# Second mixer: the context keys' gates to the context's end, by a scan on VectorE in place of eight levels on GpSimd

## The chip, the cores and the metric

The kernel runs on one core of a Trainium2 chip. The metric is the device time of one execution in microseconds (us), as the median of several runs. The engines are called as the profile calls them: PE (TensorE matmul), PEld (its weight loads), DVE (VectorE), ACT (ScalarE), POOL (GpSimd) and SP (the queue that issues most transfers).

## The reference

The network has four layers (two blocks of two) over 256 context tokens and 256 latent tokens of width 1024. The change is in the second mixer, a gated linear recurrence in two directions, with eight heads of width 128. Only the latent tokens' output is needed there.

```python
def _directional_scan(q, k, v, g, n_ctx, reverse):
    """One scan direction: context scanned alone from a zero state, latent scan starts from the final context state."""
...
    o_ctx, s_ctx = _chunk_gla(seg(q, c_sl), seg(k, c_sl), seg(v, c_sl), seg(g, c_sl), s0)
    o_lat, _ = _chunk_gla(seg(q, t_sl), seg(k, t_sl), seg(v, t_sl), seg(g, t_sl), s_ctx)
...
def _odd_mixer(h_ctx, h_lat, w_in, lower_bounds, layer, out_norm, ctx_out):
...
    for d, f in enumerate((f_fwd, f_bwd)):
        log_f = jnp.logaddexp(jnp.log(lb[d]), jnp.log1p(-lb[d]) + jax.nn.log_sigmoid(_heads(f, HGRN_HEADS).astype(jnp.float32)))
        k = -jnp.expm1(log_f)
        dirs.append(_directional_scan(q, k, i, log_f, n_ctx, reverse=(d == 1)))
    o_lat = _gated_readout(dirs[0][1] + dirs[1][1], og[:, :, n_ctx:], out_norm)
```

Here `_chunk_gla` is the recurrence S_t = diag(exp(g_t)) S_{t-1} + k_t v_t^T, o_t = S_t^T q_t. For a latent token, each context key therefore counts with the product of all gates that stand between it and the end of the context (for the reverse direction, its beginning), for each of the 128 features of its head.

## The kernel before

Activations are kept feature by feature (128 partitions) with tokens along the row. The linear layers work in fp32 split in two: for every weight tile that a transfer brings (`raw`), ACT rounds a high part (`hi`, L195) and DVE subtracts it from the tile to get the low part (`lo`, L196); PE then makes three products (L205 to L207, or L277 to L280 where tokens are the output's rows).

`odd_mixer` handles the eight heads as four pairs. `proj(p)` makes the gates of pair p for the latent (`al`) and the context tokens (`ac`), the keys `Kl` and `Kc` (one minus the gate, L814 and L816 on DVE), and the queries `q`; `late(p)` makes the output gates and the values. `hgrn_pair` then does the recurrence of one pair. Its latent part runs over eight levels of a dyadic tree. At each level, ACT gathers keys (`KC`, L898), PE multiplies keys by queries (L901), DVE puts the masked result into the score tile `S` (L903), and DVE multiplies the gates of the level into `Q2` (L915) and `Kl` (L906). DVE also makes the next level's products of neighbouring gates (`tot`, L921). The next level's matmuls need the `Q2` of the level before.

Beside this, POOL runs the same tree over the context: at each level L916 multiplies into `Kc` the gates of the level, and L921 makes the next products from `ac`. After eight levels, every context key holds all gates up to the context's end; L936 and L937 multiply `Kc` by the queries. POOL also makes `ks`, the sum of both directions' keys (L881), at the head of a pair.

The program's order is proj(0), late(0), proj(1), pair 0, late(1), proj(2), pair 1, proj(3), and then pairs 2 and 3 taking turns level by level, with late(2) and late(3) after twelve steps. The tile framework lays out each engine's instructions from this order, but lets an instruction that is ready pass earlier ones that are not. So the `tot` products and the context's levels of a pair, which depend only on its gates, stand in the queues of DVE and POOL right behind its projection, ahead of the levels of the pair before.

Of the kernel before, what the change touches and what calls it, by code (L numbers as in the profile page):

```python
# [9 lines left out]
F32 = mybir.dt.float32  # L10
# [3 lines left out]
ALU = mybir.AluOpType  # L14
# [3 lines left out]
P = 128  # L18
# [19 lines left out]
def vw(ap, off, dims):  # L38
    return bass.AP(ap.tensor, ap.offset + off, [ap.ap[0]] + [list(d) for d in dims])
# [89 lines left out]
class Kern:  # L129
# [741 lines left out]
    def hgrn_pair(self, p, al, ac, Kl, Kc, Q2, q, V, sog, gain, mix):  # L871
        nc = self.nc
        mm = nc.tensor.matmul
        DS = 512

        def g2(name):
            return mix.tile([P, 2, 256], F32, tag=name, name=self.n(name), bufs=2)

        S = g2("S")
        ks = mix.tile([P, 2, 256], F32, tag="S256", name=self.n("ks"), bufs=2)  # L880
        nc.gpsimd.tensor_tensor(ks, Kl[:, 0], Kl[:, 1], ALU.add)  # L881
        ps = self.psum("pa")
        for h in range(2):
            for tt in range(2):
                ts = slice(tt * P, (tt + 1) * P)
                mm(ps[:, h * 256 + tt * P:h * 256 + (tt + 1) * P], ks[:, h, ts], q[:, h, ts], start=True, stop=True)
        nc.scalar.copy(S.rearrange("p h n -> p (h n)"), ps)
        for d in range(2):
            nc.vector.tensor_tensor(Q2[:, d], q, al[:, d], ALU.mult)
        tl = al.rearrange("p d h n -> p (d h n)")  # L890
        tc_ = ac.rearrange("p d h n -> p (d h n)")
        for lev in range(8):
            m = 1 << lev
            nb = DS // (2 * m)
            pat = [[2 * m, nb], [DS + m, 2], [1, m]]
            if lev < 7:
                KC = g2("KC").rearrange("p h n -> p (h n)")
                nc.scalar.copy(vw(KC, 0, [[2 * m, nb], [m, 2], [1, m]]), vw(Kl, 0, pat))  # L898
                ps = self.psum("pa")
                for b in range(4):  # L900
                    mm(ps[:, b * P:(b + 1) * P], KC[:, b * P:(b + 1) * P],  # L901
                       vw(Q2, b * P, [[2 * m, 64 // m], [DS + m, 2], [1, m]]), start=True, stop=True)
                nc.vector.copy_predicated(S.rearrange("p h (t i) -> p (h t) i", t=2),  # L903
                                          self.masks[:, lev, None, :].to_broadcast([P, 4, P]),
                                          ps.rearrange("p (t i) -> p t i", t=4))
                nc.vector.tensor_tensor(vw(Kl, 0, pat), vw(Kl, 0, pat), self.dyadic(m, DS, nb, tl, "k"), ALU.mult)  # L906
            else:
                S128 = g2("S128")
                ps = self.psum("pa")
                for h in range(2):  # L910
                    o = h * 256
                    mm(ps[:, o + P:o + 256], Kl[:, 0, h, :P], Q2[:, 1, h, P:], start=True, stop=True)
                    mm(ps[:, o:o + P], Kl[:, 1, h, P:], Q2[:, 0, h, :P], start=True, stop=True)
                nc.scalar.copy(S128.rearrange("p h n -> p (h n)"), ps)
            nc.vector.tensor_tensor(vw(Q2, 0, pat), vw(Q2, 0, pat), self.dyadic(m, DS, nb, tl, "q"), ALU.mult)  # L915
            nc.gpsimd.tensor_tensor(vw(Kc, 0, pat), vw(Kc, 0, pat), self.dyadic(m, DS, nb, tc_, "k"), ALU.mult)  # L916
            if lev < 7:
                for w, eng in (("l", nc.vector), ("c", nc.gpsimd)):
                    t2 = mix.tile([P, 2, nb], F32, tag=f"tot{w}{lev}", name=self.n("tot"), bufs=2)
                    pr = vw(tl if w == "l" else tc_, 0, [[DS // m, 2], [2, nb], [1, 2]])  # L920
                    eng.tensor_tensor(t2, pr[:, :, :, 0], pr[:, :, :, 1], ALU.mult)  # L921
                    t2 = t2.rearrange("p d n -> p (d n)")
                    if w == "l":
                        tl = t2
                    else:
                        tc_ = t2
            yield
        tag = "pl" if p > 1 else "pb"
        ss = self.psum("pb")
        oS = []  # L930
        for h in range(2):
            ps = self.psum(tag)
            for j in range(2):
                js = slice(j * P, (j + 1) * P)
                o = ps[:, j * 256:(j + 1) * 256]
                mm(o, Kc[:, 0, h, js], Q2[:, 1, h], start=True, stop=False)  # L936
                mm(o, Kc[:, 1, h, js], Q2[:, 0, h], start=False, stop=True)  # L937
            S256 = mix.tile([P, 512], F32, tag="S256", name=self.n("S256"), bufs=2)
            nc.scalar.copy(S256, ps)
            po = self.psum("pa")  # L940
            vs = slice((2 * p + h) * P, (2 * p + h + 1) * P)
            for j in range(2):
                mm(po[:, :256], V[:, j, vs], S256[:, j * 256:(j + 1) * 256], start=j == 0, stop=False,
                   skip_group_check=True)
            for tt in range(2):
                ts = slice(tt * P, (tt + 1) * P)
                mm(po[:, ts], V[:, 2 + tt, vs], S[:, h, ts], start=False, stop=False, skip_group_check=True)
                mm(po[:, ts], V[:, 3 - tt, vs], S128[:, h, ts], start=False, stop=True, skip_group_check=True)
            oS.append(self.gated_readout_rows(po[:, :256], h, gain, mix, ss))
            yield  # L950
        r = self.sm.tile([P, 8], F32, tag="rs16", name=self.n("rs"))
        self.rstd_rows(ss[:, :4], P, 4, r[:, :4])
        yield
        for h in range(2):
            bc = self.psum(tag)
            for tt in range(2):
                mm(bc[:, tt * P:(tt + 1) * P], r[:, tt * 2 + h:tt * 2 + h + 1].to_broadcast([P, P]), self.ident,
                   start=True, stop=True)
            hd = 2 * p + h
            nc.vector.tensor_tensor(oS[h], oS[h], bc[:, :256], ALU.mult)  # L960
            nc.gpsimd.tensor_tensor(sog[:, hd], oS[h], sog[:, hd], ALU.mult)
# [1172 lines left out]
```

## Time and profile before

| | |
|---|---|
| median of 3 runs | 2568.2 us (2568.14 to 2576.02) |
| the profiled execution's own time | 2566.27 us |
| its span in the trace | 2563.7 us |
| PE busy | 2414.7 us (94%) |
| DVE busy | 1518.1 us (59%), 2897 instructions |
| ACT busy | 971.3 us (38%) |
| POOL busy | 503.0 us (20%), 648 instructions |
| mean granted clock of PE | 0.966 |

A busy share says how long an engine had an instruction in work. PE's share is near full, so that what counts is where PE is idle and which engine it waits for there. The second mixer lies between about 890 and 1185 us of the span. The profiled execution's own time is 2.6 us above its span, which is what lies around it, and 1.9 us below the median of the runs.

### The profile page before, as it was taken

The numbers are of one execution on the slowest core, as the hardware profiler recorded it, in microseconds if no ns is written. First come the engines' busy times: TensorE is split into PE (matmuls) and PEld (weight loads), VectorE is DVE, ScalarE is ACT, GpSimd is POOL, SyncE is SP. The second block draws the span as 40 slices with busy tenths as digits, with TensorE's granted clock in tenths as the row PEclk, the third lists the DMA queues.
The fourth block names the chain that finished last, engine by engine and source line by source line (L and its number), as shares of the span: only waits on it lengthen the run. The fifth ranks groups of instructions, "written<-read, shape, count | busy, mean of one in ns | idle before, by whom it ended". The sixth has DMA issues, their size and how long they took to land.

```text
span 2563.7 us, 40161 instructions
## 1 busy us (share of the span) xinstructions
PE 2414.7 (94%) x15813; PEld 1970.4 (77%) x15813; DVE 1518.1 (59%) x2897; ACT 971.3 (38%) x1591; POOL 503.0 (20%) x648
## 2 busy tenths in 40 slices
PE   6999989999999998889999999999999999948999
PEld 5885566888888688887799696546888888627999
DVE  5545436777853656673655533654688734585666
ACT  5523323322222433333444444443423224534543
POOL 2810012556630233230100100110100000360000
PEclk8999999999999999999999999989999999989999
DMA  8326673555552332123855431003365533976554
GB/s 279 122 95 230 226 279 108 160 163 167 161 145 91 106 124 67 59 82 136 282 178 182 154 110 60 9 17 105 111 188 181 165 99 104 200 254 212 156 181 149
DMA packets 162924, 378.04 MB, mean 147 GB/s; under 512 B 24144, under 2 KB 70096, under 8 KB 162608
## 3 DMA queue, kind: packets, MB, share of 16 engines
q1 hardware_dynamic: 159728, 368.27, 45.0%
q0 software_dynamic: 3008, 7.21, 1.0%
q8 instruction: 124, 2.03, 0.3%
q14 instruction: 64, 0.52, 0.1%
HBM read 344.75 MB, written 30.67 MB: 146 GB/s over the span
## 4 chain that ended last, share of the span: by engine, by line
PE 79%; DVE 10%; DMA 4%; ACT 3%; issue 2%; POOL 1%; SPq 0%; DVEq 0%; ACTq 0%; POOLq 0%
PE pl L205 18%; PE pl L206 18%; PE pl L207 17%; PE pm L329 3%; PE pl L984 2%; PE pa L77 2%; DVE lo L196 2%; DMA mcol<-ada_t 2%; PE pl L279 1%; PE pl L280 1%; DVE pm L395 1%; PE pl L277 1%; PE pb L77 1%; PE pa L661 1%; PE pl L1006 1%
## 5 line engine op out<-in xcount | busy, mean ns | idle before, releaser
L195 ACT CAST hi<-raw 128x1024 fp32r<-128x1024 f32 (+4 forms) x393 | 400.4, 1020 | 847.1 <-PE pl L206 555.0
L196 DVE TENSOR_TENSOR lo<-raw,hi 128x1024 fp32r<-128x1024 f32 (+4 forms) x393 | 496.6, 1265 | 332.2 <-ACT hi L195 330.2
L206 PE MATMUL pl<-X,hi 128*128 128x256 f32 (+1 forms) x2032 | 649.2, 321 | 6.2 <-POOL X L490 5.7
L205 PE MATMUL pl<-X,hi 128*128 128x256 f32 (+1 forms) x2032 | 651.3, 322 | 1.8 <-ACT X L487 1.8
L207 PE MATMUL pl<-X,lo 128*128 128x256 f32 (+1 forms) x2032 | 647.6, 320 | 0.8 <-DVE lo L196 0.7
L206 PEld LDWEIGHTS pl<-X,hi 128*128 128x128 f32 x2032 | 392.6, 194 | 37.4 <-POOL X L490 8.7
L205 PEld LDWEIGHTS pl<-X,hi 128*128 128x128 f32 x2032 | 391.9, 194 | 36.3 <-issue 6.9
L207 PEld LDWEIGHTS pl<-X,lo 128*128 128x128 f32 x2032 | 392.5, 193 | 31.5 <-issue 4.9
L206 PE MATMUL pl<-hl,hi 128*128 128x256 f32 (+1 forms) x1071 | 326.8, 306 | 6.7 <-DVE hl L1713 6.6
L205 PE MATMUL pl<-hh,hi 128*128 128x256 f32 (+1 forms) x1071 | 329.5, 309 | 3.4 <-ACT hh L1712 3.2
L207 PE MATMUL pl<-hh,lo 128*128 128x256 f32 (+1 forms) x1071 | 325.9, 305 | 0.0
L205 PEld LDWEIGHTS pl<-hh,hi 128*128 128x128 f32 x1071 | 202.4, 189 | 25.6 <-issue 7.1
L206 PEld LDWEIGHTS pl<-hl,hi 128*128 128x128 f32 x1071 | 202.6, 189 | 18.9 <-DVE hl L1713 8.7
L207 PEld LDWEIGHTS pl<-hh,lo 128*128 128x128 f32 x1071 | 202.7, 189 | 10.5 <-issue 0.4
L205 PE MATMUL pl<-M,hi 128*128 128x256 f32 (+1 forms) x416 | 125.4, 303 | 7.4 <-ACT hi L195 6.4
L1505 POOL TENSOR_TENSOR Ec<-PGr,bc 128x576 f32<-128x576 f32 x64 | 95.5, 1503 | 169.8 <-DMA bc<-s_w 89.0
L329 PE MATMUL pm<-mraw,s_cc 128*32 128x512 f32 x576 | 115.7, 606 | 11.3 <-DMA mraw<-ada_w 10.9
L207 PE MATMUL pl<-M,lo 128*128 128x256 f32 (+1 forms) x416 | 122.2, 295 | 1.2 <-DVE lo L196 1.2
L206 PE MATMUL pl<-M,hi 128*128 128x256 f32 (+1 forms) x416 | 122.8, 296 | 0.2 <-DVE M L856 0.2
L1726 DVE TENSOR_TENSOR y<-y,pl 128x256 f32<-128x256 f32 (+1 forms) x86 | 45.1, 525 | 115.9 <-PE pl L207 115.5
L490 POOL TENSOR_TENSOR X<-nt,X 128x256 fp32r<-128x256 f32 x48 | 37.5, 781 | 382.7 <-ACT nt L489 382.7
L395 DVE SCALAR_TENSOR_TENSOR pm<-mcol,mrow 128x512 f32<-128x512 f32 x128 | 89.2, 697 | 34.0 <-DMA mcol<-ada_t 21.7
(515 smaller groups left out, 3753.5 us busy)
## 6 DMA issues: line engine op xcount, KB each, us to landing
mraw<-mod_w SPq DMA_DIRECT2D x96, 512.0 KB, 5.5
raw<-f_u SPq DMA_DIRECT2D x88, 512.0 KB, 4.3
mraw<-ada_w SPq DMA_DIRECT2D x64, 512.0 KB, 6.3
raw<-p_u SPq DMA_DIRECT2D x64, 512.0 KB, 3.7
raw<-p_d SPq DMA_DIRECT2D x64, 512.0 KB, 3.6
raw<-ow_fm SPq DMA_DIRECT2D x32, 512.0 KB, 3.3
mcol<-ada_t SPq DMA_DIRECT2D x64, 256.0 KB, 3.0
raw<-f_d SPq DMA_DIRECT2D x32, 448.0 KB, 3.3
```

What stands on the lines that cost most here:

```text
L77: K.nc.tensor.matmul(self.ps[32 * j:32 * j + 32, :N], K.ones[:rows, :32], self.sq[:rows, :N], start=k < 4, stop=k + 4 >= self.kt, skip_gro ...
L195: nc.scalar.copy(hi, raw)
L196: nc.vector.tensor_tensor(lo, raw, f32(hi), ALU.subtract)
L205: mm(out, w[0][:, kw, wsl], xh, start=first and a == 0, stop=False, skip_group_check=True)
L206: mm(out, w[0][:, kw, wsl], xl, start=False, stop=False, skip_group_check=True)
L207: mm(out, w[1][:, kw, wsl], xh, start=False, stop=last and a == nk - 1, skip_group_check=True)
L329: nc.tensor.matmul(ps[32 * j:32 * j + 32, :], s[:, k, :], raw[:, jj * 512:(jj + 1) * 512], start=k == 0, stop=k == KT - 1, skip_group_chec ...
L395: nc.vector.scalar_tensor_tensor(self.psum("pm"), buf[:, n % 2], 1.0, s[:, v], ALU.mult, ALU.mult, accum_out=(dst if h else part)[:, v, j: ...
L490: nc.gpsimd.tensor_tensor(lo[:, k, a:b], t, f32(hi[:, k, a:b]), ALU.subtract)
L984: nc.tensor.matmul(ps[:, :nk], q[:, tt * P:(tt + 1) * P], k[:, :nk], start=True, stop=True)
L1505: nc.gpsimd.tensor_tensor(Ec[i], ff[i], cs[i], ALU.mult)
L1726: nc.vector.tensor_tensor(y[:, c, a0:b0], y[:, c, a0:b0], ps, ALU.add)
```

## The change

POOL's eight levels over the context go. In place of them, DVE scans the context's gates `ac` in place: for each head and direction one `tensor_tensor_scan` over 255 tokens, whose state is multiplied by each gate in turn (and by a column of ones, which changes nothing). For one direction it goes forwards, for the other backwards. Two scans (both heads) of one direction are issued at level 3, those of the other at level 5. After each two, one multiplication on POOL puts the products into `Kc`. The latent part's tree and its `tot` products on DVE stay as they were.

```diff
-        tc_ = ac.rearrange("p d h n -> p (d h n)")
         for lev in range(8):
...
             nc.vector.tensor_tensor(vw(Q2, 0, pat), vw(Q2, 0, pat), self.dyadic(m, DS, nb, tl, "q"), ALU.mult)
-            nc.gpsimd.tensor_tensor(vw(Kc, 0, pat), vw(Kc, 0, pat), self.dyadic(m, DS, nb, tc_, "k"), ALU.mult)
             if lev < 7:
-                for w, eng in (("l", nc.vector), ("c", nc.gpsimd)):
-                    t2 = mix.tile([P, 2, nb], F32, tag=f"tot{w}{lev}", name=self.n("tot"), bufs=2)
-                    pr = vw(tl if w == "l" else tc_, 0, [[DS // m, 2], [2, nb], [1, 2]])
-                    eng.tensor_tensor(t2, pr[:, :, :, 0], pr[:, :, :, 1], ALU.mult)
-                    t2 = t2.rearrange("p d n -> p (d n)")
-                    if w == "l":
-                        tl = t2
-                    else:
-                        tc_ = t2
+                t2 = mix.tile([P, 2, nb], F32, tag=f"totl{lev}", name=self.n("tot"), bufs=2)
+                pr = vw(tl, 0, [[DS // m, 2], [2, nb], [1, 2]])
+                nc.vector.tensor_tensor(t2, pr[:, :, :, 0], pr[:, :, :, 1], ALU.mult)
+                tl = t2.rearrange("p d n -> p (d n)")
+            if lev in (3, 5):
+
+                d = lev // 2 - 1
+                for h in range(2):
+                    a = vw(ac, d * DS + h * 256 + 255 * d, [[1 - 2 * d, 255]])
+                    nc.vector.tensor_tensor_scan(a, a, self.ones[:, :1].to_broadcast([P, 255]), 1.0, ALU.mult, ALU.mult)
+                ks, gs = slice(1 - d, 256 - d), slice(d, 255 + d)
+                nc.gpsimd.tensor_tensor(Kc[:, 1 - d, :, ks], Kc[:, 1 - d, :, ks], ac[:, d, :, gs], ALU.mult)
             yield
```

## Rows read from the trace of the kernel before

**Rows 1.** Waits of PE, 890 to 1180 us: total, times, longest (us).
```profile
PE pa L901 <- DVE Q L915: 15.3, 3, 7.5
PE pa L901 <- DVE S L903: 8.1, 1, 8.1
PE pl L279 <- DVE lo L196: 3.7, 1, 3.7
PE pl L207 <- DVE lo L196: 0.7, 1, 0.7
```

**Rows 2.** Busy time by stretch: first, second, fourth wait, each with the stretch behind.
```profile
core 0: us, PE busy (x) PEld busy (x) DVE busy (x) ACT busy (x) POOL busy (x), PEclk, DMA share, GB/s
913.00:920.60 7.60, 3.19 (x26) 2.83 (x24) 7.53 (x9) 2.27 (x4) 7.60 (x5) 0.98 0.22 69
920.60:924.00 3.40, 3.40 (x17) 3.40 (x18) 3.40 (x4) 0.86 (x2) 3.40 (x3) 0.54 0.49 154
969.80:977.30 7.50, 0.02 (x1) 0.00 (x1) 7.36 (x10) 0.00 (x0) 7.42 (x9) 0.84 0.38 117
977.30:982.00 4.70, 4.67 (x23) 4.70 (x24) 4.70 (x6) 1.46 (x2) 2.06 (x2) 0.52 0.09 37
...
1102.50:1110.60 8.10, 0.03 (x1) 0.00 (x0) 8.00 (x10) 0.53 (x1) 8.10 (x9) 0.63 0.22 65
1110.60:1115.50 4.90, 4.89 (x25) 4.89 (x26) 4.90 (x5) 1.30 (x2) 4.78 (x4) 0.56 0.00 0
```

**Rows 3.** DVE in order of time, second wait: start, duration, operation.
```profile
962.74 1.13 DVE L814 TENSOR_SCALAR Kc<-sg,lbt 128x256 f32<-128x256 f32 x1
...
964.49 2.55 DVE L921 TENSOR_TENSOR tot<-al 128x512 f32<-128x512 f32 x1
...
967.50 2.56 DVE L196 TENSOR_TENSOR lo<-raw,hi 128x1024 fp32r<-128x1024 f32 x1
...
975.02 0.71 DVE L903 COPY_PREDICATED S<-masks,pa 128x512 f32<-128x512 int32 x1
975.63 1.55 DVE L915 TENSOR_TENSOR Q<-Q,al 128x512 f32<-128x512 f32 x1
...
980.52 0.68 DVE L915 TENSOR_TENSOR Q<-Q,tot 128x512 f32<-128x512 f32 x1
981.12 0.68 DVE L906 TENSOR_TENSOR Kl<-Kl,tot 128x512 f32<-128x512 f32 x1
```

**Rows 4.** POOL in order of time, second wait: the first of its 15 instructions.
```profile
962.58 1.14 POOL L921 TENSOR_TENSOR tot<-ac 128x512 f32<-128x512 f32 x1 [33.66 <-DVE ac L816]
```

**Rows 5.** Single lines: duration least/median/most (ns), first and last start.
```profile
L814 DVE TENSOR_SCALAR Kc<-sg,lbt x16: 344/348/1170, 895.8 to 1095.8; 128x256 f32<-128x256 f32 x16
L670 DVE TENSOR_TENSOR tot<-gla_a x2: 679/804/929, 92.0 to 98.3; 128x512 f32<-128x512 f32 x2
L684 DVE TENSOR_TENSOR K<-K,tot x2: 425/425/425, 228.3 to 239.6; 128x256 f32<-128x256 f32 x2
L196 DVE TENSOR_TENSOR lo<-raw,hi x393: 426/1225/3689, 42.8 to 2552.4; 128x1024 fp32r<-128x1024 f32 x171, 128x896 fp32r<-128x896 f32 x16, 128x672 fp32r<-128x672 f32 x4, 128x544 fp32r<-128x544 f32 x4
L916 POOL TENSOR_TENSOR Kc<-Kc,tot x28: 1052/1320/4903, 912.7 to 1113.5; 128x512 f32<-128x512 f32 x28
```

**Rows 6.** DVE in order of time, fourth wait: `Kc`, eleven more, then `S`.
```profile
1095.78 1.13 DVE L814 TENSOR_SCALAR Kc<-sg,lbt 128x256 f32<-128x256 f32 x1
...
1109.84 0.71 DVE L903 COPY_PREDICATED S<-masks,pa 128x512 f32<-128x512 int32 x1
```

**Rows 7.** Waits of SP's queue, 890 to 1000 us.
```profile
SPq L257 <- DVE lo L196: 77.7, 16, 10.5
...
SPq L326 <- PE pm L329: 4.1, 1, 4.1
```

**Rows 8.** Busy time of one stretch among the levels.
```profile
984.00:986.00 2.00, 2.00 (x19) 1.89 (x18) 2.00 (x4) 0.41 (x1) 0.00 (x0) 1.00 0.00 0
```

## Prediction

> **What bounds the kernel now.** I read the page first: PE is busy for 94% of the span, so a change on DVE and POOL can pay only where PE stands still. I therefore asked next for PE's own waits in the second mixer. Four places make up nearly all of them [rows 1]: one wait of 3.7 us (with 0.7 us just ahead) for a `lo`, two of 7.5 us for `Q`, and one of 8.1 us for `S`. All four are waits for DVE. The reader should see that none is a wait for POOL: nobody on PE waits for the context's levels, and counted by waits POOL's work is free.
>
> The view by stretches shows what the waits have in common [rows 2]. In each, DVE is busy throughout and so is POOL, while PE is at work for 3.19 of 7.6 us in the first and for about nothing in the others (the third, at 1045, repeats the second in every column to within 0.03 us and isn't shown). PE's idle time there is 4.4 + 7.5 + 7.5 + 8.1 = 27.5 us. [...] That costs 3.4 x 0.46 = 1.6 us, 4.7 x 0.48 = 2.3 us, the same for the third, and 4.9 x 0.44 = 2.2 us: 8.4 us more. All four together are 35.9 us. This is the most that a cure of these waits could give.
>
> Why is DVE late? The order of time in the second wait tells it [rows 3, 4]. POOL starts on the context's levels at 962.58, as soon as the gates are there, and works almost without a pause until 979.4 (2.06 us into the stretch behind the wait [rows 2]). In that time the same DVE instructions that are short elsewhere are long. A `lo` takes 2.56 us, against a median of 1.22; a `Q` takes 1.55 us, and 0.68 once POOL has stopped; `Kc` takes 1.13 us, against 0.35; the first `tot` takes 2.55 us, where the other mixer's instruction of the same shape took as little as 0.68 [rows 3, 5]. The copy under a mask, which reads its data from PSUM, takes 0.71 us in the middle of it. So DVE's products of two SBUF tensors, and some copies with a factor, wait for POOL's instructions, and PE waits for DVE. POOL's levels are not free after all.
>
> **What is removed.** For each pair, eight multiplications into `Kc` (L916) and seven products (L921) leave POOL: 60 instructions in four pairs. For the second wait, I go through DVE's queue from 962.74 to the start of `S` at 975.02, which is 12.3 us [rows 3]. Undisturbed, `Kc` and `Kl` are 0.35 each; the first `tot` is 0.68; the six smaller ones halve in length each time, and I put them at 1.5 together (0.42, 0.29, 0.23, 0.19, 0.18, 0.17: 0.16 fixed, the rest in proportion, an estimate from the 0.68); two `lo` are 2.45. That is 5.3 us. Successive starts lie about 0.07 closer than the durations (0.60 for an instruction of 0.68 [rows 3]), which takes 0.7 off. DVE thus gets back 7.7 us, and `Q` right behind another 0.9.
>
> **What is added.** Four scans for each pair, sixteen in all. No row shows a scan. The nearest rows bound it: a plain product of 256 columns takes 0.43 us, and the dearest instruction with 256 results in this stage is the `tot` held up by POOL, 2.55 us [rows 3, 5]. I take 0.68, the undisturbed `tot` with its 256 results, since a scan must hand each result on and should be no faster than the slower kind of product. Four make 2.7 us. The framework will put them where the `tot` products are now, right behind the projection, as they too need only the gates; I count all four ahead of `S`, although an instruction of an earlier pair that is ready may pass them.
>
> [...]
>
> POOL keeps two multiplications of 510 columns for each pair. Undisturbed, L916 takes 1.05 us on 512 columns [rows 5]. Each can hold up one DVE instruction by between nothing and its whole length. I take half for each, 1.0 us for both. They wait for DVE's scans, which POOL's levels did not; queued behind them on POOL are only `ks` and the readout's product, and POOL would have been busy there anyway. `Kc` itself is wanted by L936 only some 20 us later.
>
> [...]
>
> **The sum.** Second wait: 7.7 + 0.9 - 2.7 - 1.0, and 0.3 for closer starts of the scans, makes 5.2 us, and 2.3 of the 7.5 us stay. Of the 2.3 us for the clock I count half. The mean clock over the waits was 0.84 in the second and 0.63 in the fourth [rows 2]; between full and half that means that it fell some 5 us after PE had stopped in the one, 2 us in the other, so a wait of 2 to 3 us may or may not lower it. That is 6.3 us. The third wait is the same row of instructions, 6.3 us. The fourth has 14.1 us of DVE work ahead of its `S` [rows 6]: `Kc` and `Kl` 0.70, six `tot` 1.99 (all but the smallest), one `lo` 1.22, a product into `Kl` 0.68 and two for `Q` 1.36, together 5.95, and 0.8 off for closer starts is 5.2 us. So 8.9 + 0.9 - 3.7 makes 6.1 of the 8.1, and half the clock 1.1: 7.2 us. In the first, POOL and DVE do the same for its pair, and I take the same net, 7.7 - 3.7 = 4.0 us, which is more than the 3.7 waited for; that wait goes, with most of the 0.7 ahead of it. I count 3.7 us and the clock's 1.6: 5.3 us. Together 25.1 us.
>
> Does it reach the end? Between the waits PE is full, so time that it gains is kept, unless a transfer is late. The mixer's weights are issued as `lo` frees their buffers, and the background weights as PE does [rows 7]; both would move forward along with the cause. The profiled execution took 2566.3 us; less 25.1 is 2541.2, and the median of the runs lies 1.9 above it: 2543 us.
>
> **Rivals.** *All four waits vanish.* If the scan costs 0.43 us, or the framework lets `S` pass two scans, the waits shrink to about 1 us and the clock stays up: 2568.2 - 31 to 35, or 2533 to 2537 us. For it: PE itself finishes the preceding matmuls only at about 968, so DVE needs to be early by little. Against: four scans and two multiplications are still 3.7 us.
>
> *A part is taken back.* The scans, or one of the multiplications, land among the levels, where DVE has no slack (busy 2.00 of 2.00 us while PE is, too [rows 8]), or a new order in the queues brings a wait somewhere else. Four scans of 0.68 in each pair's levels, and the full 2.1 us for both multiplications, are 2.7 + 2.1 = 4.8 us for each of four pairs, 19 of the roughly 35 us: 2552 us, and with one more wait of several us, about 2560.
>
> *The gain does not come.* DVE's added work equals what it gets back. The point is where four scans and the multiplications eat the 8.6 us of the second wait: (8.6 - 1.0) / 4 = 1.9 us for each scan. Near it the time stays at 2568.
>
> *Slower.* The scan is dear: it goes through its elements one after the other, and costs, held up or not, as much as the dearest row, 2.55 us. Four are 10.2 us, so each wait grows by 10.2 + 1.0 - 8.6 = 2.6 us, four by 10.4: 2579 us. Against it: even in the dearest rows most is the wait for POOL, which goes.
>
> **How the numbers follow.** My own sum, with 17 to 30 us gained, gets 0.50 (2538 to 2551 us); all waits gone 0.17; a part taken back 0.14 (2551 to 2560); no gain 0.11; slower 0.08. A measurement of this kernel can tell about 0.3%, or 7.7 us, from no change. Faster by more is therefore 0.50 + 0.17 + 0.14 = 0.81, the same 0.11, slower 0.08. The range reaches from the first rival's middle, 2533, to the end of the second, 2560. This leaves out the last two and the far end, about 0.2. As the cases of a gain hold most of the chance on one side, the likeliest one's own range, 2538 to 2551, stands inside.
>
> **What the profile would show.** Right: POOL's row of instructions at the four places gone except two multiplications and `ks`; DVE's `tot<-al` near 0.7 us, no `lo` of 2.5 us there; PE's four waits at 0 to 3 us each; scans near 0.7 us, ahead of `S`; the granted clock in the stretches behind the waits near 1. Wrong: scans above 1.5 us; DVE's instructions as long as before without POOL beside them (then POOL was not the cause); the scans standing between the levels, with PE waiting for `Q` or `S` there; or the four waits gone and PE waiting for transfers instead.

## The result, and the profile after

The changed kernel takes 2536.4 us (median of 4 runs, 2529.59 to 2547.7) against 2568.2 us before (4 runs, 2565.15 to 2576.02). The ratio is 0.9876, with a 95% interval of 0.9832 to 0.992. The interval of the ratio means 20.5 to 43.1 us less. In a second timing, beside the last experiments, it took 2538.0 us (6 runs) against 2560.6 before, a ratio of 0.991 (0.9892 to 0.9928), or 22.6 us less. The profiled execution took 2539.8 us, with a span of 2538.0.

For what follows I use one measure more, as medians of the same kernel differ by several us between timings: the *mixer's stretch*, in the profiled execution, from the start of the first gate product's sigmoid (L810) to the end of the last rounding of the mixer's outputs (L855). Outside it, the profiled executions differ by up to 10 us on either side without an edit there, so that differences of the medians below 5 us say little. The view by stretches, over the mixer's stretch before, and then after:

```profile
894.50:1185.80 291.30, 260.91 (x1895) 245.76 (x1894) 188.50 (x291) 111.64 (x179) 83.78 (x72) 0.95 0.23 77
```

```profile
891.00:1158.30 267.30, 258.36 (x1895) 241.42 (x1894) 165.96 (x307) 111.75 (x180) 27.17 (x20) 0.99 0.25 83
```

The columns are those of [rows 2]. The stretch is 24.0 us shorter; the sum in the prediction was 25.1. PE's idle time falls from 30.4 to 8.9 us (21.5 us), and its busy time by 2.5 us, at a mean granted clock of 0.99 in place of 0.95. POOL loses 56.6 us of busy time; DVE, which has 16 instructions more, is 22.5 us less busy.

PE's waits after, 885 to 1160 us, against [rows 1] (L900, L902, L914, L918 answer to L901, L903, L915, L921 before):

```profile
PE pa L900 <- DVE Q L914: 2.6, 2, 1.3
PE pa L900 <- DVE S L902: 2.1, 1, 2.1
PE pa L900 <- ACT KC L897: 1.6, 3, 0.8
...
PE pl L279 <- DVE lo L196: 0.3, 1, 0.3
```

The four places are still there, in the same order, but they hold 0.3, 1.3, 1.3 and 2.1 us, 5.0 in place of 27.5. DVE in order of time at the second place, against [rows 3]:

```profile
954.81 0.35 DVE L814 TENSOR_SCALAR Kc<-sg,lbt 128x256 f32<-128x256 f32 x1
955.07 0.35 DVE L814 TENSOR_SCALAR Kl<-sg,lbt 128x256 f32<-128x256 f32 x1
955.33 0.68 DVE L918 TENSOR_TENSOR tot<-al 128x512 f32<-128x512 f32 x1
955.94 0.68 DVE L925 TENSOR_TENSOR_SCAN ac<-ac,ones 128x255 f32<-128x255 f32 x1
956.53 1.20 DVE L196 TENSOR_TENSOR lo<-raw,hi 128x1024 fp32r<-128x1024 f32 x1
957.65 2.60 DVE L918 TENSOR_TENSOR tot<-tot 128x256 f32<-128x256 f32 x6
960.19 1.22 DVE L196 TENSOR_TENSOR lo<-raw,hi 128x1024 fp32r<-128x1024 f32 x1
961.33 0.72 DVE L902 COPY_PREDICATED S<-masks,pa 128x512 f32<-128x512 int32 x1
961.95 1.11 DVE L914 TENSOR_TENSOR Q<-Q,al 128x512 f32<-128x512 f32 x1
```

From `Kc` to `S` there are 6.5 us, where there were 12.3. The first `tot` takes 0.68 us and not 2.55, a `lo` 1.2 and not 2.56. Only one scan stands in the queue here; the other three of the pair passed ahead into gaps of the projection (939.23, 944.21 and 949.97). POOL at that time:

```profile
956.70 2.51 POOL L927 TENSOR_TENSOR Kc<-Kc,ac 128x510 f32<-128x510 f32 x1 [4.88 <-DVE ac L925]
```

The same at the fourth place: first DVE, then POOL.

```profile
1073.71 1.45 DVE L918 TENSOR_TENSOR tot<-tot 128x256 f32<-128x256 f32 x1
1075.08 2.29 DVE L196 TENSOR_TENSOR lo<-raw,hi 128x1024 fp32r<-128x1024 f32 x1
```

```profile
1072.76 2.12 POOL L881 TENSOR_TENSOR ks<-Kl 128x512 f32<-128x512 f32 x1 [3.64 <-DVE Kl L814]
1074.84 1.45 POOL L927 TENSOR_TENSOR Kc<-Kc,ac 128x510 f32<-128x510 f32 x1
```

What was left on POOL still holds DVE up: the `tot` beside `ks` ends 0.3 us behind it and takes 1.45 us, against 0.43 with memsets on POOL; the `lo` beside the multiplication ends 1.1 us behind it, nearly the whole length of a `lo` without POOL (1.22 us), and takes 2.29 us. PE's clock, by stretches of 2 us at the second and the fourth place:

```profile
962.00:964.00 2.00, 0.80 (x7) 0.83 (x8) 2.00 (x4) 0.00 (x0) 0.00 (x0) 1.00 0.71 258
964.00:966.00 2.00, 2.00 (x18) 1.89 (x17) 1.73 (x4) 1.18 (x2) 0.00 (x0) 1.00 0.01 4
...
1080.00:1082.00 2.00, 1.33 (x8) 1.33 (x9) 2.00 (x3) 0.00 (x0) 0.00 (x0) 1.00 0.02 8
1082.00:1084.00 2.00, 2.00 (x12) 2.00 (x11) 1.79 (x3) 0.67 (x1) 0.00 (x0) 0.52 0.00 0
1084.00:1086.00 2.00, 2.00 (x13) 2.00 (x13) 1.32 (x3) 0.62 (x1) 0.00 (x0) 0.63 0.00 0
```

It stays at 1.00 at the second place, and at the third too, and falls to 0.52 and 0.63 only behind the fourth. In a second profile of the changed kernel, taken with the last experiments, PE waits for `S` at the fourth place for the same 2.1 us, and the clock stays at 1.00 over the whole stretch:

```profile
891.00:1157.60 266.60, 257.12 (x1895) 239.99 (x1895) 165.94 (x307) 111.72 (x180) 27.18 (x20) 1.00 0.26 84
```

So the fall behind the fourth place comes in one execution of this kernel and not in another.

### The profile page after: what moved, and what is told of

Read it like the earlier page. It is cut to its first block, busy times and chain, and to the rows that moved or that the text cites. A ratio compares the mean times of both kernels' runs of the same rounds, so it can differ in the third digit from the quotient of the medians.

```text
span 2538.0 us, 40121 instructions
## 1 busy us (share of the span) xinstructions
PE 2409.9 (95%) x15813; PEld 1961.7 (77%) x15813; DVE 1497.5 (59%) x2913; ACT 972.0 (38%) x1591; POOL 447.8 (18%) x596
## 4 chain that ended last, share of the span: by engine, by line
PE 78%; DVE 11%; DMA 5%; ACT 3%; issue 2%; POOL 1%; SPq 0%; DVEq 0%; ACTq 0%; POOLq 0%
PE pl L205 18%; PE pl L206 17%; PE pl L207 17%; PE pm L329 3%; PE pl L985 2%; DVE lo L196 2%; PE pa L77 2%; DMA mcol<-ada_t 1%; PE pl L279 1%; PE pl L280 1%; PE pl L277 1%; PE pb L77 1%; DVE pm L395 1%; PE pa L661 1%; PE pb L1016 1%
## 5 line engine op out<-in xcount | busy, mean ns | idle before, releaser
L196 DVE TENSOR_TENSOR lo<-raw,hi 128x1024 fp32r<-128x1024 f32 (+4 forms) x393 | 486.5, 1239 | 330.0 <-ACT hi L195 328.0
L329 PE MATMUL pm<-mraw,s_cc 128*32 128x512 f32 x576 | 119.5, 624 | 10.8 <-DMA mraw<-ada_w 10.4
```

Of the source, the lines that this page charges most:

```text
L196: nc.vector.tensor_tensor(lo, raw, f32(hi), ALU.subtract)
L329: nc.tensor.matmul(ps[32 * j:32 * j + 32, :], s[:, k, :], raw[:, jj * 512:(jj + 1) * 512], start=k == 0, stop=k == KT - 1, skip_group_chec ...
```

## The experiments

The theory of the prediction (A) is that POOL's levels hold up DVE's products of two SBUF tensors, and DVE holds up PE. Against it stand two rivals. The first (B): the gain comes from the order, for the framework did lay out PE's and ACT's instructions anew when the scans came, and not from POOL. The second (C): the scan makes the gain, since it does in four instructions what took a tree of fifteen.

**Neither levels nor scans.** The context's part goes altogether.

```diff
-            if lev in (3, 5):
-                ...
-                    nc.vector.tensor_tensor_scan(a, a, self.ones[:, :1].to_broadcast([P, 255]), 1.0, ALU.mult, ALU.mult)
-                ...
-                nc.gpsimd.tensor_tensor(Kc[:, 1 - d, :, ks], Kc[:, 1 - d, :, ks], ac[:, d, :, gs], ALU.mult)
```

> Left out: the context keys' gates altogether (no levels on POOL, no scans, no multiplications into Kc), so this is the removal alone. Theory A (DVE's products wait for POOL's instructions, PE waits for DVE): all four waits of PE stay at 0 to 1.5 us, the mixer's stretch from the first gate's sigmoid to the last rounding of its output, 291.3 us before and 267.3 us after the change, is 261 to 267 us, and the time is 0 to 6 us below the changed kernel's. If the scans and multiplications had a real price on the path, as my 3.7 us for each pair said, it is nearer to 8 to 12 us below the changed kernel's. Theory B (the new order of the queues made the gain, not the lack of POOL's work): the stretch can be anywhere from 255 to 290 us.

Measured: 2531.1 us, ratio 0.9875 (0.9846 to 0.9905). The mixer by stretches:

```profile
889.80:1148.20 258.40, 254.07 (x1896) 239.21 (x1895) 152.86 (x291) 111.80 (x180) 13.91 (x12) 1.00 0.26 86
```

The order on PE, ACT, DVE and SP is that of the kernel before, instruction for instruction, and yet the stretch is 32.9 us shorter than before. So the order is not the cause (against B). The ceiling in the prediction was 35.9. The changed kernel's stretch is 8.9 us longer than this one: that is the price of all that the change adds. The stretch lies below the 261 to 267 us that I expected, a range that puts this price at 6 us or less; 8.9 us fit the other branch, in which the additions have a real price. By its ratio alone (0.9875 against 0.9876) this kernel can't be told from the changed one.

**Scans, and POOL's levels again.** POOL does its fifteen instructions for each pair once more, with results that nobody reads.

```diff
+            nc.gpsimd.tensor_tensor(vw(Kd, 0, [[2 * m, nb], [m, 2], [1, m]]), vw(Kc, 0, pat), self.dyadic(m, DS, nb, tc_, "k"), ALU.mult)
             if lev < 7:
+                t3 = mix.tile([P, 2, nb], F32, tag=f"totc{lev}", name=self.n("totc"), bufs=1)
+                pr = vw(tc_, 0, [[DS // m, 2], [2, nb], [1, 2]])
+                nc.gpsimd.tensor_tensor(t3, pr[:, :, :, 0], pr[:, :, :, 1], ALU.mult)
```

> The changed kernel, to which POOL's fifteen instructions for each pair come back as an idle load: same sizes, they read Kc and the latent gates and write scratch tiles that nobody reads. The order of instructions on PE, DVE, ACT and SP is the changed kernel's, line by line. Theory A: the four waits come back to 7 us and more each, as DVE has the scans beside them; DVE's first tot is 2.5 us again; the mixer's stretch is 288 to 302 us against 267.3, the time 2560 to 2575 us. Theory B (the new order made the gain): DVE and PE have that order here too, so the stretch stays at 265 to 272 us and the time at about 2536 us.

Measured: 2572.0 us, ratio 1.0036 (1.0021 to 1.0051). The mixer by stretches, then PE's waits in it, then two of DVE's instructions at the second place:

```profile
888.40:1188.20 299.80, 264.26 (x1896) 246.81 (x1895) 198.46 (x307) 111.68 (x181) 98.61 (x80) 0.95 0.23 74
```

```profile
PE pa L902 <- DVE Q L916: 18.7, 5, 8.1
PE pa L902 <- DVE S L904: 7.6, 1, 7.6
PE pl L279 <- DVE lo L196: 5.2, 1, 5.2
```

```profile
960.71 2.54 DVE L925 TENSOR_TENSOR tot<-al 128x512 f32<-128x512 f32 x1
...
966.61 4.59 DVE L925 TENSOR_TENSOR tot<-tot 128x256 f32<-128x256 f32 x6
```

The order is that of the changed kernel, and the four waits are back in full, with no wait for POOL. The first `tot` takes 2.54 us again. POOL's load thus costs 32.5 us in the new order (299.8 against 267.3) and 32.9 in the old one (291.3 against 258.4), and the additions cost 8.5 us with the load (299.8 against 291.3) and 8.9 without. The two effects add up, and what POOL's load costs doesn't depend on the order; the 8.5 and 8.9 us hold the additions and the new order together.

**A load that reads nothing.** Is it that POOL is busy, or what it reads? Here memsets take the place of the levels; first two for every product of either kind, with a write to the `tot` tiles too:

```diff
+            for _ in range(2):
+                nc.gpsimd.memset(vw(Kc, 0, pat), 0.5)
...
+                        eng.memset(t2, 0.5)
+                        eng.memset(t2, 0.5)
```

> The kernel before, in which each multiplication and product of POOL's levels is replaced by two memsets of the same output, which read nothing from SBUF (left out: the context's gates in Kc, which holds a constant). The order on DVE, ACT and SP is the one of before, line by line. Theory A in its narrow form (DVE's second SBUF input waits for POOL's reading): DVE's instructions are as short as without POOL, the stretch is 262 to 270 us against 291.3 before, though POOL is busy for about as long. Theory A in its wide form (any work of POOL holds up DVE): the stretch stays at 285 to 292 us. Theory B (it is the order): the order is that of before, so the stretch stays at about 291 us, with short DVE instructions.

Measured: 2534.6 us, ratio 0.9885 (0.9851 to 0.9919). The mixer by stretches:

```profile
891.10:1156.40 265.30, 257.00 (x1895) 240.91 (x1894) 158.54 (x291) 111.80 (x181) 57.19 (x117) 0.99 0.26 84
```

POOL was busy for 57.19 us, less than before, and the memsets of `tot`, which wait for nothing, ran ahead of the mixer's first gates, where they held one instruction of DVE:

```profile
L788 DVE TENSOR_SCALAR lbt<-lbt x1: 6061/6061/6061, 890.7 to 890.7; 128x16 f32<-128x16 f32 x1
```

It takes 0.17 us in the other kernels (the three numbers are least, median and most, in ns). The first gates waited for it, ACT's sigmoid for the gates, and PE 3.9 us for the `hi` that ACT rounds behind that, so these 3.9 us of the stretch come from the misplaced memsets. The load lay in part in the wrong place, so I made it again: four memsets of 512 columns for each multiplication, none for `tot`.

```diff
+            for _ in range(4):
+                nc.gpsimd.memset(vw(Kc, 0, pat), 0.5)
```

> The kernel before, POOL's levels replaced by four memsets for each multiplication and nothing for the products, so that POOL is at work in each place for 16 to 20 us, as long as before, but reads nothing (left out: the context's gates in Kc). The order on all other engines is that of before, line by line. Narrow theory A (DVE's second SBUF input waits for POOL's reads): DVE's products of two SBUF tensors keep their short times, the stretch is 257 to 266 us against 291.3 us, as in the run without any levels (258.4). Wide theory (any work of POOL holds up DVE): 285 us and more; the shorter memsets of the run before had POOL at work for 10 us in each place and would then have hidden it. Copies with a factor (Kc, Kl, the gates) may be held up, as one of 0.17 us took 6.06 us there.

Measured: 2532.6 us, ratio 0.987 (0.9836 to 0.9905). The mixer by stretches, then POOL at the second place, then DVE there:

```profile
896.30:1155.40 259.10, 254.23 (x1896) 239.22 (x1895) 153.66 (x291) 111.87 (x180) 89.97 (x140) 1.00 0.26 86
```

```profile
958.73 21.20 POOL L917 MEMSET Kc<- 128x512 f32 x32 [26.01 <-DVE Kc L814]
```

```profile
958.85 0.69 DVE L922 TENSOR_TENSOR tot<-al 128x512 f32<-128x512 f32 x1
959.57 0.43 DVE L922 TENSOR_TENSOR tot<-tot 128x256 f32<-128x256 f32 x1
959.91 1.22 DVE L196 TENSOR_TENSOR lo<-raw,hi 128x1024 fp32r<-128x1024 f32 x1
961.05 1.18 DVE L922 TENSOR_TENSOR tot<-tot 128x128 f32<-128x128 f32 x5
962.39 1.23 DVE L196 TENSOR_TENSOR lo<-raw,hi 128x1024 fp32r<-128x1024 f32 x1 [0.16 <-ACT hi L195]
963.72 0.75 DVE L903 COPY_PREDICATED S<-masks,pa 128x512 f32<-128x512 int32 x1
```

POOL is busier than before (89.97 against 83.78 us) and at the same places, in the order of the kernel before on PE, DVE, ACT and SP; still DVE's products are as short as if it were alone, and the stretch is within 0.7 us of the one without any load. So in these runs it is POOL's instructions that read SBUF, not its being busy, that hold DVE's products up: beside the reading levels the first `tot` takes 2.54 to 2.55 us and a `lo` up to 2.56, beside the memsets 0.69 and 1.23.

The `lbt` above is a copy with a factor and was held by memsets all the same. The run with long memsets shows this again: two copies with a factor start beside the third row of memsets (1025.3 to 1046.4), and take 0.76 and 0.69 us where the same two take 0.41 us in the kernel without the context's part.

```profile
1043.44 0.76 DVE L816 TENSOR_SCALAR ac<-sg,lbt 128x256 f32<-128x256 f32 x1
1044.12 0.69 DVE L816 TENSOR_SCALAR al<-sg,lbt 128x256 f32<-128x256 f32 x1
```

So memsets held up these copies, though not the products. What sets the two apart, no run here shows.

**The levels on DVE.** The tree as it was, without a scan, all on DVE. Theory C has it slow.

```diff
-            nc.gpsimd.tensor_tensor(vw(Kc, 0, pat), vw(Kc, 0, pat), self.dyadic(m, DS, nb, tc_, "k"), ALU.mult)
+            nc.vector.tensor_tensor(vw(Kc, 0, pat), vw(Kc, 0, pat), self.dyadic(m, DS, nb, tc_, "k"), ALU.mult)
...
-                for w, eng in (("l", nc.vector), ("c", nc.gpsimd)):
+                for w, eng in (("l", nc.vector), ("c", nc.vector)):
```

> The kernel before with the context's levels moved from POOL to DVE as they are, sixty instructions, without a scan. Theory A: nothing holds up DVE, but it gets about 29 us of work (thirty-two of 0.68 us and twenty-eight of 0.17 to 0.68 us) where the scans add 10.9 us. In each of the four waits that is 7 us for what 7.7 us had been lost: the waits shrink by 0 to 4 us only where the order lets them stand ahead of PE's needs, the stretch is 272 to 290 us, the time 2540 to 2566 us. If the scan itself made the gain, it stays at before's 2568 us or goes above it.

Measured: 2535.7 us, ratio 0.9898 (0.9869 to 0.9927). The mixer by stretches:

```profile
895.70:1163.30 267.60, 257.78 (x1895) 241.89 (x1894) 177.59 (x351) 111.73 (x180) 12.10 (x12) 0.99 0.25 83
```

The stretch is as long as with scans (267.3), below what I expected. So C falls: to get the work off POOL is the whole gain, and the scan is one way to do it among others. DVE carries 24.7 us more than in the kernel without the context's part, yet the stretch is only 9.2 us longer (5.5 us of PE's idle time, 3.7 of its busy time).

**Each scan twice.** A second scan into a spare tile ahead of each, to price the scan.

```diff
+                    nc.vector.tensor_tensor_scan(sx[:, :255], a, self.ones[:, :1].to_broadcast([P, 255]), 1.0, ALU.mult, ALU.mult)
                     nc.vector.tensor_tensor_scan(a, a, self.ones[:, :1].to_broadcast([P, 255]), 1.0, ALU.mult, ALU.mult)
```

> The changed kernel with each scan made twice, the added one into a scratch tile: sixteen more instructions of 0.68 us on DVE, 10.9 us. If scans are hidden in the slack of the projections, where the changed kernel's trace has two or three of each pair's four, only one or two of each pair cost anything: the mixer's stretch grows from 267.3 us by 2 to 5 us. If a scan lies on the path wherever it stands, as my sum counted it, by 8 to 11 us.

Measured in a single run: 2549.7 us. The mixer by stretches:

```profile
893.60:1172.80 279.20, 261.77 (x1895) 244.46 (x1894) 176.86 (x323) 111.85 (x179) 27.59 (x20) 0.98 0.25 80
```

DVE is 10.9 us busier than in the changed kernel and the stretch 11.9 us longer, a little more than the 8 to 11 expected: these scans lie on the path. Of the 11.9 us, 8.5 are idle time of PE; the other 3.4 are busy time, at a mean clock of 0.98 against 0.99. At the second place four scans now stand ahead of `S`, where there was one. It stays open why 24.7 us of levels on DVE cost 9.2 us of the stretch, and the 24.0 us by which DVE is busier here than without the context's part (176.86 - 152.86; the doubled scans, and what the multiplications on POOL hold up) cost 20.8. The place in DVE's queue is the likely reason: at the second place the queue from `Kc` to `S` takes 5.9 us with the levels and 7.4 with the doubled scans, as more of the levels' products stand behind `S`. No run here separates this from the multiplications that stayed on POOL.

**What is left on POOL.** Either the two multiplications, or `ks`, or both move to DVE.

```diff
-        nc.gpsimd.tensor_tensor(ks, Kl[:, 0], Kl[:, 1], ALU.add)
+        nc.vector.tensor_tensor(ks, Kl[:, 0], Kl[:, 1], ALU.add)
...
-                nc.gpsimd.tensor_tensor(Kc[:, 1 - d, :, ks], Kc[:, 1 - d, :, ks], ac[:, d, :, gs], ALU.mult)
+                nc.vector.tensor_tensor(Kc[:, 1 - d, :, ks], Kc[:, 1 - d, :, ks], ac[:, d, :, gs], ALU.mult)
```

The multiplications alone:

> The changed kernel with the two multiplications into Kc of each pair on DVE instead of POOL; the sum of keys stays on POOL. Theory A: DVE gets eight instructions of 0.68 us, 5.4 us, and loses the holding up by 12.2 us of POOL's work, of which the trace of the changed kernel shows about 3 us behind the second and third place (a Q of 1.1 us, a tot row of 2.6 us) and 2 us behind the fourth. The mixer's stretch, 267.3 us in the changed kernel, is 264 to 268 us, the time within 3 us of the changed kernel's. If POOL's reading is the only price of the additions, it falls to 260 us.

Measured: 2534.6 us, ratio 0.9886 (0.987 to 0.9901), a stretch of 263.7 us, just under the range expected. The sum `ks` alone:

> The changed kernel with the sum of keys alone moved to DVE (four instructions), the multiplications still on POOL. Theory A: the fourth place, where PE waits 2.1 us and then runs at the lower clock for some 4 us, gets 2 to 3 us back, the first gets little, as PE hardly waits there now. The stretch is 263 to 266 us.

Measured: 2538.1 us, ratio 0.9893 (0.9878 to 0.9909), a stretch of 264.9 us. Both:

> As e5, and the sum of keys on DVE too, so that POOL has only the readout's product in the mixer. Theory A: in the changed kernel the sum took 2.1 to 3.7 us on POOL in the first and the fourth place and held up a tot, a lo and a Kl by 3 to 4 us there; on DVE it costs 0.68 us. The stretch is 260 to 265 us, the time 2 to 8 us below the changed kernel's. If DVE's own work is what is left on the path, it stays at 265 to 269 us.

Measured: 2536.1 us, ratio 0.9878 (0.9856 to 0.9899), a stretch of 263.1 us. As this is the shortest of those that compute everything, I timed it again beside the changed kernel, on one chip:

> The changed kernel once more, beside the next one on the same chip: 2530 to 2545 us, stretch 266 to 268 us. It shows how far executions of one kernel lie apart outside the mixer.

> The version with nothing of the context and no sum of keys on POOL again, timed in more rounds: its stretch was 263.1 us against 267.3, so theory A expects 4 us less than the changed kernel beside it. That is less than the executions of one kernel differ among themselves, so the times may well not tell the two apart; the stretch should, at 262 to 264 us.

Measured: the changed kernel 2538.0 us, ratio 0.991 (0.9892 to 0.9928), its stretch 266.6 us; nothing on POOL 2533.5 us, ratio 0.9896 (0.9872 to 0.992), its stretch again 263.1 us:

```profile
889.60:1152.70 263.10, 256.90 (x1894) 239.85 (x1894) 167.23 (x319) 111.77 (x179) 6.58 (x8) 1.00 0.26 85
```

Twelve more instructions on DVE make it only 1.3 us busier, since POOL no longer holds up the others. The stretch is 3.5 to 4.2 us shorter in both profiles, but the times overlap: by its time this version can't be told from the changed kernel.

## Why the prediction was right, point by point

**The cause** was right. The same load costs 32.5 to 32.9 us in either order, and 0.7 us when it only writes (259.1 against 258.4). The waits' own sum, 35.9 us, was a little too high as a ceiling (32.9): without the context's part, at a mean clock of 1.00, PE is busy 6.8 us less than before (260.91 against 254.07), where I had worked out 8.4 us for the clock.

**What DVE gets back** was close. Undisturbed, the queue from `Kc` to `S` is 5.4 us at the second place (958.33 to 963.72 with memsets on POOL); I had 5.3 less 0.7, or 4.6, so that DVE got 0.8 us less back than I took. The `tot` and the `lo` have the durations that I took. `Q<-Q,al` behind `S` takes 1.11 us and not 0.68, so that the "another 0.9" was 0.4.

**The scan** was right in its size. The single lines after, in ns, least, median and most:

```profile
L925 DVE TENSOR_TENSOR_SCAN ac<-ac,ones x16: 658/680/687, 894.0 to 1073.1; 128x255 f32<-128x255 f32 x16
L927 POOL TENSOR_TENSOR Kc<-Kc,ac x8: 1089/1214/2507, 900.7 to 1074.8; 128x510 f32<-128x510 f32 x8
L881 POOL TENSOR_TENSOR ks<-Kl x4: 1275/1696/3682, 905.6 to 1072.8; 128x512 f32<-128x512 f32 x4
```

It takes 0.68 us in either direction. So the rival of a dear scan (1.9 us for no gain, 2.55 for slower) fell with its price.

**Two terms were off, and their errors cancel in part.** I counted four scans ahead of `S`, 2.7 us, and one stood there, 0.7. What I had wrong is where the scans stand: `S` did not pass scans, as the first rival had it, but three of the four ran earlier, in gaps of the projection, as soon as their gates were there. Against that, I took 1.0 us for what both multiplications hold up, half of a range that was my estimate, and left out `ks`. At the second place one multiplication stretched the six smaller `tot` from 1.61 us (with memsets) to 2.60, so that 1.0 is right for that place, though not as half a length for each: this one cost DVE about its whole length alone (1.09 us), and the other of the pair met no instruction of DVE (950.73, in a gap). At the fourth, `ks` and a multiplication together stretched a `tot` and a `lo` by 2.1 us (1.45 + 2.29 against 0.43 + 1.22). The queue from `Kc` to `S` came to 6.5 us at the second place (my terms gave 12.3 - 7.7 + 2.7 + 1.0 - 0.3 = 8.0), and to 7.9 at the fourth (1071.98 to 1079.91; my terms gave 14.1 - 8.9 + 3.7 = 8.9, without the 0.3 us for closer starts that the second place has).

**What stays of the waits** was forecast as about 0.7, 2.3, 2.3 and 2.0 us, and is 0.3, 1.3, 1.3 and 2.1. A new wait of 1.6 us for ACT's `KC`, in three parts, takes some of it back: the idle time falls by 22.5 at the four places, 0.6 more at a product into `Kl`'s scores (L912 before), less 1.6, which is the 21.5 measured. I had 20.2.

**The clock** was forecast to cost half as much in three places. What it cost before, 8.4 us, is worked out from the clocks behind the waits in [rows 2]. In steps of half a microsecond that profile has 1.00 up to 974.5 us and 0.50 from 975.0 to 981.5 at the second place, and 1.00 up to 1104.5 and 0.50 from 1105.0 to 1114.5 at the fourth, which is the full and half that the prediction counts with. In the profile after, the clock came back at the second and the third and fell behind the fourth, where it costs about 1.7 us. By these rows it should have given more than the 5.0 us forecast, and yet PE's busy time fell by only 2.5 us. Of the difference, 1.0 us is that the 16 matmuls of the background weights (L329) overlap less: two of them now run ahead by themselves, and the 16 keep PE busy for 4.2 us in place of 3.2. The 224 matmuls of the levels (L900) are busy for 34.0 us, against 32.4 without the context's part, which holds the clock's loss in part. The rest isn't traced. So the sum's 25.1 us come close to the measured 24.0 partly by luck: the waits gave back 1.3 us more than it said, and PE's busy time 2.5 us less.

**Does it reach the end?** Yes: PE waits only 0.2 us for a transfer in the stretch, in which transfers take 0.25 of the queues' time in place of 0.23. The profiled execution is 26.5 us shorter than that of before, 24.0 of them in the mixer. The median, 2536.4, lies below the likeliest case's own range of 2538 to 2551, and inside that of "all four waits vanish"; yet the waits are those of my own sum. The 31.8 us between the first medians are more than the mixer gives; the second timing gave 22.6. I put the difference down to how executions vary outside the mixer, which the spread of the medians bears out, but no run shows its cause.

## What to carry to other kernels

A helper engine that nobody waits for can still set the pace: look whether instructions of another engine are longer while it works (here a `tot` of 2.55 us in place of 0.68), in order of time, before its work is called free. Here it paid to move such work to the engine that was late, whether as a scan or as the old tree, because what was taken from POOL gave DVE back more than it added: its busy time in the stretch fell from 188.50 us to 165.96 with scans and to 177.59 with the tree. To tell such contention from a change of order, leave the order and put in the helper's place a load that only writes.

## What the runs showed of the hardware

- POOL is stretched as well: the sum `ks` of 512 columns takes 1.28 us at least and up to 3.68 where DVE's products run beside it (905.64 us in the changed kernel: a `lo` and a `tot` beside it kept their 1.22 and 0.42 us, the next `tot` took 1.32).
- A product with the first level's gates, `Q<-Q,al`, takes 1.11 us with POOL idle (961.95 us in the changed kernel). One of the same 512 columns with a later level's `tot` takes 0.68, and `Q<-q,al` (L889), which takes its 512 columns of `al` one after the other, 0.67 (963.49 us), so that here the number of columns alone did not set the duration.
- A `tensor_scalar` of 16 columns was held for 6.06 us, against 0.17, by a row of short memsets on POOL, and ended as they did (896.72 us, the last of them at 896.69); products of two SBUF tensors of the same 16 columns (L786, L787) took 0.17 us each beside the same row. Beside longer memsets, two `tensor_scalar` of 256 columns took 0.76 and 0.69 us, against 0.41.
